# A 3x3 convolution on one core: two blocks in a turn of TensorE's loop, and the context ended ahead of the wait for the last stores

## The chip, the cores and the metric

The kernel runs on one core of a Trainium2 chip. The metric is the device time of one execution in microseconds (us); the figure for a kernel is the median of several runs. A profile is one execution recorded by the hardware profiler; its *span* runs from the first to the last recorded instruction, and the execution's own device time is a little longer than the span.

## The reference

A batch of 16 images with 64 channels of 64 x 64 points is convolved with 128 filters of 3 x 3, with one row and column of zeros around each image. Everything is float32 in memory.

```python
batch, c_in, h, w, c_out = 16, 64, 64, 64, 128
x_pad = np.pad(x, ((0, 0), (0, 0), (1, 1), (1, 1)), mode='constant')
output[b, co] += weight[co, ci, kh, kw] * x_pad[b, ci, kh:kh+h, kw:kw+w]   # over ci, kh, kw
```

The input is 16.8 MB, the output 33.6 MB.

## The kernel before

**Tiling.** Two images make a pair p (0 to 7): their 2 x 64 channels fill the 128 partitions. A pair is computed in four blocks of 16 output rows, so there are 32 blocks n = 4p + blk. The 16 output rows of a block are 8 even and 8 odd ones.

**The trick in the rows.** Along the rows, pairs of output rows share work. With the row taps g0, g1, g2 of the filter, the kernel keeps five weight sets in `Wt`: G1, and G0, G2, G21 = g2 - g1 and G01 = g0 - g1. For each block TensorE makes three groups of sums, each for both images (b2 = 0, 1), a bank of PSUM for each image:
- group 0 (shared): G1 on the sums of two neighbouring rows (`ss`), 3 column taps x 2 images = 6 matmuls;
- group 1 (even rows): G21 on one row set and G0 on the row above, 12 matmuls from `xs`;
- group 2 (odd rows): G01 and G2 (the row below), 12 matmuls from `xs`.

A matmul uses 64 of the 128 rows of the array, one image's channels, and those of the two images alternate. It has 8 rows x 64 columns, or 63 for the outer column taps. At an image's top G0 would read a row above it, at its bottom G2 one below; there, these six matmuls have 7 rows.

**The engines' parts.** TensorE (PE) runs the 30 matmuls of each block (L294). POOL makes the sums `ss` (L115; the first two blocks' by DVE). ACT copies group 0's banks to `ut` in SBUF (L204), then casts the rows of the next block to float16 in `xs` (L121). DVE adds `ut` to the even and the odd rows' banks and writes the float32 result (L234): four adds of 512 columns in a block, the even rows' (i = 0) for both images first, then the odd ones'. Finished pairs are stored from `homes`, one store for each image (2 MB) and two of 1 MB for the last pair's; image 0's by SP's queue, image 1's by ACT's (L109). Pairs 0 to 3 are loaded by SP as float32 into `homes`, pairs 4 to 7 by POOL's queue with a cast to float16 (L95), at points given by `LOADS`. Nine `homes` of 2 MB serve as inputs first and then as outputs, so a first add of a pair may have to wait for an earlier store (`gate_out`).

**The order.** It is written out by hand with semaphores. `s_pe`, `s_act` and `s_dve` count what the engines have finished; `tiles(n, k)` is the count at which the k-th bank of block n is done, `copies(n, k)` and `adds(n, k)` the like for ACT and DVE. TensorE alone runs a hardware loop (L263: 8 turns of four blocks, with `hint_back_edge=True`), and since a loop can't wait for growing counts it takes credits: `c_sum` (a block's sums), `c_cast` (its cast), `c_bank` (a pair of banks was read out by DVE: one after the even adds, one after the odd adds, except the last), each lowered by 1 at L273. `c_bank` starts at 3.

**The banks.** A block's six banks are `(6n + 2g + b2) % 8`, so groups walk in a ring of four pairs. Group 0 of block n takes the pair that the odd adds of block n-2 read, group 2 the one that the even adds of block n-1 read; group 1's pair was freed by ACT's copies ahead of `c_cast`.

**The places of rows and sums.** `xs` holds all 64 rows of a pair, `ss` 32 sums; a block's cast covers the rows of `CUTS` (18, 16, 16, 14 rows). POOL mostly sums two blocks in one instruction.

**The end.** Stores whose home is not used again count up `s_end`. After the critical section closes (L73), SP waits for `s_end` (L306), and then the context ends (L332): the engines meet in barriers, and POOL clears the range of semaphores.

Of the kernel before, what the change touches and what calls it, by code (L numbers as in the profile page):

```python
# [6 lines left out]
F16 = mybir.dt.float16  # L7

NP = 8
NB = 4  # L10
RB = 8
H = W = 64
CO = 128
TILES = 6
G0, G21, G1, G01, G2 = range(5)
# [3 lines left out]

PIECES = [(0, 32), (0,), (0,), (0,), (0,), (0,), (0, 32), (0, 32, 50)]  # L20

LOADS = {6: [(6, 0), (6, 1)], 8: [(7, 0)], 10: [(7, 1), (7, 2)]}
CUTS = [(0, 18), (18, 34), (34, 50), (50, 64)]


def kernel(tc: tile.TileContext, x: bass.AP, weight: bass.AP, out: bass.AP):
    nc = tc.nc
# [3 lines left out]
    def sem(name):  # L31
        return tc.alloc_semaphore(name)

    def sbuf(name, shape, dt):
        return nc.alloc_sbuf_tensor(name, shape, dt).ap()
# [3 lines left out]
    s_in = [[sem(f"s_in{p}{k}") for k in range(len(PIECES[p]))] for p in range(NP)]  # L39
    s_pe = sem("s_pe")  # L40
    s_act = sem("s_act")
    s_dve = sem("s_dve")
    s_out = {}
    s_end, s_done = sem("s_end"), sem("s_done")

    c_sum, c_cast, c_bank = sem("c_sum"), sem("c_cast"), sem("c_bank")

    def tiles(n, k):
        return 3 + TILES * n + k

    def copies(n, k):
        return 3 + 2 * n + k
# [6 lines left out]
    PE, ACT, DVE, POOL, SP = nc.tensor, nc.scalar, nc.vector, nc.gpsimd, nc.sync  # L59
# [10 lines left out]
    def when(inst, s, count):  # L70
        return inst.wait_op(s, count, "sem-ge")

    with tc.tile_critical(sync_engine=EngineType.Pool):  # L73
        homes = [sbuf(f"home{k}", [128, H, W], F32) for k in range(9)]
        pairs = homes[:4] + [sbuf(f"pair{p}", [128, H, W], F16) for p in range(4, NP)]
        xs = sbuf("xs", [128, H, W], F16)
        ss = sbuf("ss", [128, H // 2, W], F16)
        uts = [[sbuf(f"ut{k}{b}", [128, RB, W], F32) for b in range(2)] for k in range(2)]
        w_raw = sbuf("w_raw", [CO, 64 * 9], F32)
        w16 = sbuf("w16", [CO, 64 * 9], F16)  # L80
# [1 line left out]
        zeros = sbuf("zeros", [128, 512], F16)  # L82
        ident = sbuf("ident", [128, 128], F16)
        banks = [nc.alloc_psum_tensor(f"bank{k}", [128, RB, W], F32).ap() for k in range(8)]
# [5 lines left out]
        def rows(t):  # L90
            return t.rearrange("p (j i) c -> p j i c", i=2)

        def load(eng, p, k):
            lo, hi = (PIECES[p] + (H,))[k : k + 2]
            eng.dma_start(  # L95
                pairs[p][:, lo:hi, :], x_rows[128 * p : 128 * p + 128, lo:hi, :]
            ).then_inc(s_in[p][k], 16)
# [4 lines left out]
        def arrived(eng, name, p, hi):  # L102
            for k, lo in enumerate(PIECES[p]):
                if lo < hi and (name, p, k) not in seen:
                    seen.add((name, p, k))
                    eng.wait_ge(s_in[p][k], 16)
# [3 lines left out]
                out[2 * p + b2, :, lo:hi, :], homes[OUT_HOME[p][b2]][:, lo:hi, :]  # L110
            ).then_inc(s, 16)

        def sums(eng, lo, n, p):
            v = rows(pairs[p])
            return eng.tensor_add(  # L115
                ss[:, lo : lo + n, :], v[:, lo : lo + n, 0, :], v[:, lo : lo + n, 1, :]
            )

        def cast(m):
            lo, hi = CUTS[m % NB]  # L120
            return ACT.copy(xs[:, lo:hi, :], pairs[m // NB][:, lo:hi, :])  # L121


        gate_out = {}
        pieces, n_end = {}, 0
# [47 lines left out]
        when(POOL.tensor_copy(w16, w_raw), s_w, 16).then_inc(s_pool, 1)  # L173
        POOL.wait_ge(s_dve, 2).then_inc(c_sum, 1)
        POOL.wait_ge(s_dve, 3).then_inc(c_sum, 1)
        arrived(POOL, "pool", 0, H)
        load(POOL, 4, 0)
        sums(POOL, 2 * RB, 2 * RB, 0).then_inc(c_sum, 2)
        for k in range(2, 2 * NP):
            p = k // 2  # L180
            lo = 2 * RB * (k % 2)
            n = RB if k == 2 * NP - 1 else 2 * RB
            arrived(POOL, "pool", p, 2 * (lo + n))
            if k == 4:
                load(POOL, 5, 0)
            when(sums(POOL, lo, n, p), s_pe, tiles(2 * k - 3, 2)).then_inc(c_sum, n // RB)
            if n == RB:
                arrived(POOL, "pool", p, H)
                sums(POOL, lo + n, n, p).then_inc(c_sum, 1)
            for q, piece in LOADS.get(k, ()):  # L190
                load(POOL, q, piece)


        wp_bank = {G1: 4, G2: 5, G0: 6}
        for i, g in enumerate((G1, G2, G0)):
            when(
                ACT.copy(wrow(g), flat[wp_bank[g]][:, 0 : 3 * CO]), s_pe, i + 1  # L197
            ).then_inc(s_act, 1)
        arrived(ACT, "act", 0, CUTS[0][1])
        cast(0).then_inc(c_cast, 1)  # L200
        for n in range(NB * NP):
            for b2 in range(2):
                when(
                    ACT.copy(uts[n % 2][b2], banks[(6 * n + b2) % 8]), s_pe, tiles(n, 1 + b2)  # L204
                ).then_inc(s_act, 1)
            m = n + 1
            if m < NB * NP:
                arrived(ACT, "act", m // NB, CUTS[m % NB][1])
                cast(m).then_inc(c_cast, 1)
            done = n - 1  # L210
            if done >= 0 and (done // NB, 1, done % NB) in pieces:
                p = done // NB
                ACT.wait_ge(s_dve, adds(n, 1))
                store(ACT, p, 1, *pieces[p, 1, done % NB])
# [4 lines left out]
        DVE.memset(zeros, 0.0).then_inc(s_dve, 1)  # L219
        when(DVE.tensor_sub(wrow(G21), wrow(G2), wrow(G1)), s_act, 2)  # L220
        when(DVE.tensor_sub(wrow(G01), wrow(G0), wrow(G1)), s_act, 3)  # L221
        when(sums(DVE, 0, RB, 0), s_in[0][0], 16).then_inc(s_dve, 1)
        sums(DVE, RB, RB, 0).then_inc(s_dve, 1)
        for n in range(NB * NP):
            p, blk = divmod(n, NB)
            j0 = RB * blk
            for i in range(2):
                for b2 in range(2):
                    if blk == 0 and i == 0 and gate_out[p, b2] is not None:
                        DVE.wait_ge(*gate_out[p, b2])  # L230
                    if i == 0 and b2 == 0:
                        DVE.wait_ge(s_act, copies(n, 2))
                    add = when(
                        DVE.tensor_add(  # L234
                            rows(homes[OUT_HOME[p][b2]])[:, j0 : j0 + RB, i, :],
                            banks[(6 * n + 2 + 2 * i + b2) % 8],
                            uts[n % 2][b2],
                        ),
                        s_pe,
                        tiles(n, 3 + 2 * i + b2),  # L240
                    )
                    last = n == NB * NP - 1 and i == 1
                    add.then_inc(s_dve if b2 == 0 or last else c_bank, 1)
# [15 lines left out]
                    )  # L259
            mm.then_inc(s_pe, 1)  # L260
        spin(4)
        PE.sem_inc(c_bank, 3)
        with nc.Fori(0, NP, engines=(EngineType.PE,), hint_back_edge=True):  # L263
            for blk in range(NB):
                j0 = RB * blk
                groups = (
                    ([(G1, None)], (c_sum, c_bank)),
                    ([(G21, 1), (G0, -1)], (c_cast,)),
                    ([(G01, 0), (G2, 2)], (c_bank,)),
                )  # L270
                for gi, (taps, credits) in enumerate(groups):
                    for c in credits:
                        PE.wait_ge(c, 1).then_inc(c, -1)  # L273
                    acc = [banks[(6 * blk + 2 * gi + b2) % 8] for b2 in range(2)]
                    n = 3 * len(taps)
                    i = 0
                    for wi, off in taps:
                        for kw in (1, 0, 2):
                            c_lo, c_hi = max(0, 1 - kw), min(W, W + 1 - kw)
                            for b2 in range(2):  # L280
                                p0 = 64 * b2
                                lo, hi = j0, j0 + RB
                                cols = slice(c_lo + kw - 1, c_hi + kw - 1)
                                if off is None:
                                    rhs = ss[p0 : p0 + 64, lo:hi, cols]
                                else:
                                    while 2 * lo + off < 0:
                                        lo += 1
                                    while 2 * (hi - 1) + off > H - 1:
                                        hi -= 1  # L290
                                    rhs = xs[
                                        p0 : p0 + 64, 2 * lo + off : 2 * (hi - 1) + off + 1 : 2, cols
                                    ]
                                mm = PE.matmul(  # L294
                                    acc[b2][:, lo - j0 : hi - j0, c_lo:c_hi],
                                    Wt[p0 : p0 + 64, wi, kw, :],
                                    rhs,
                                    start=i == 0,
                                    stop=i == n - 1,
                                )  # L300
                                if i == n - 1:
                                    mm.then_inc(s_pe, 1)
                            i += 1

    tc.no_sync_barrier()
    SP.wait_ge(s_end, SP.to_reg(16 * n_end)).then_inc(s_done, 1)  # L306


# [28 lines left out]
```

## Time and profile before

| | |
|---|---|
| median of 3 runs | 126.46 us (126.23 to 126.65) |
| the profiled execution | 125.64 us |
| its span | 123.8 us |
| TensorE matmul busy | 108.0 us (87%) |
| DVE busy | 84.1 us (68%) |
| ACT busy | 67.2 us (54%) |
| POOL busy | 38.9 us (31%) |
| HBM read, written | 17.07 MB, 33.55 MB |

How to read the views: the rows of tenths cut the span in 40 slices of 3.1 us, a digit 9 being 90% or more. `PEclk` is the granted clock of TensorE. A row of groups has line, engine, operation, out<-in with shapes, number, and then busy time and the mean of one. A row of the timeline has the start, the length, the line and the number of instructions merged; the bracket tells the idle time before and what ended it. Rows with a q behind the engine (PEldq, SPq) are of its instruction sequencer. Matmuls overlap, so the length of a row of matmuls runs past the start of the next.

### The profile page before, as it was taken

Reading aid. Unit: us, or ns where it says so; the run is one execution under the profiler, and the core shown is the slowest. Engines: PE = TensorE matmul, PEld = TensorE weight load, DVE = VectorE, ACT = ScalarE, POOL = GpSimd, SP = SyncE. Lnnn points to the kernel's source line nnn. Section 1 sums busy time; section 2 is a strip of 40 time slices with the busy share of each in tenths; the row PEclk is TensorE's granted clock in tenths of the full one; section 3 lists DMA queues with packets and bytes.
Section 4 is the critical chain, followed back from the end, with each engine's and each line's share of the span. In section 5 each row is a group of like instructions: output and inputs, shape, how many; then the busy total and the mean of one; then the engine's idle time right before and its main releaser. Section 6 shows DMA issues by size and latency. Waiting matters only on the chain.

```text
span 123.8 us, 2533 instructions
## 1 busy us (share of the span) xinstructions
PE 108.0 (87%) x989; PEld 56.7 (46%) x989; DVE 84.1 (68%) x133; ACT 67.2 (54%) x100; POOL 38.9 (31%) x30
## 2 busy tenths in 40 slices
PE   5969999999999999999999999999999999970000
PEld 1525555555555555555555555555555555530000
DVE  0067777877787778777877787788888887771000
ACT  4266656666666666666666566656665666520000
POOL 2207457170708270615054423233241103000000
PEclk9999999999999999999999999999999999999555
DMA  4999999999999999999999999999999999999993
GB/s 108 392 442 424 365 320 326 387 296 363 365 352 344 381 396 379 392 380 389 387 392 377 388 387 381 380 395 413 383 400 412 422 383 429 432 426 416 429 426 156
DMA packets 4467, 46.46 MB, mean 375 GB/s; under 512 B 496, under 2 KB 624, under 8 KB 1264
## 3 DMA queue, kind: packets, MB, share of 16 engines
q1 hardware_dynamic: 2160, 25.46, 50.0%
q10 hardware_dynamic: 1296, 16.78, 31.7%
q0 software_dynamic: 1008, 4.19, 16.6%
q14 instruction: 3, 0.02, 0.0%
HBM read 17.07 MB, written 33.55 MB: 409 GB/s over the span
## 4 chain that ended last, share of the span: by engine, by line
PE 82%; DVE 2%; DVEq 0%; issue 0%
PE bank L294 82%; DVE home L234 2%; DVEq L73 0%
## 5 line engine op out<-in xcount | busy, mean ns | idle before, releaser
L234 DVE TENSOR_TENSOR home<-bank,ut 128x512 f32<-128x512 f32 x128 | 81.9, 686 | 21.9 <-PE bank L294 21.7
L294 PE MATMUL bank<-xs,Wt 64*128 64x504 f16 (+3 forms) x768 | 87.5, 373 | 0.0
L294 PEld LDWEIGHTS bank<-xs,Wt 64*128 64x128 f16 x768 | 43.6, 94 | 38.6
L204 ACT COPY ut<-bank 128x512 f32<-128x512 f32 x64 | 34.4, 589 | 37.7 <-PE bank L294 37.7
L115 POOL TENSOR_TENSOR ss<-pair 128x1024 f16<-128x1024 f16 (+1 forms) x9 | 17.1, 1906 | 39.1 <-PE bank L294 32.4
L294 PE MATMUL bank<-ss,Wt 64*128 64x504 f16 (+1 forms) x192 | 26.5, 377 | 1.1 <-PEq L273 1.1
L115 POOL TENSOR_TENSOR ss<-home 128x1024 f16<-128x1024 f32 x7 | 16.5, 2364 | 14.5 <-PE bank L294 12.5
L121 ACT CAST xs<-home 128x1024 f16<-128x1024 f32 (+2 forms) x16 | 16.9, 1057 | 0.3 <-DMA home<-in_x_dram 0.3
L121 ACT COPY xs<-pair 128x1024 f16<-128x1024 f16 (+2 forms) x16 | 16.9, 1059 | 0.0
L294 PEld LDWEIGHTS bank<-ss,Wt 64*128 64x128 f16 x192 | 10.8, 94 | 10.8 <-issue 1.5
L95 POOL DMA_DIRECT2D pair<-in_x_dram x7 | 4.0, 577 | 8.6 <-DMA home<-in_x_dram 8.6
L248 PE MATMUL bank<-zeros 128*128 128x512 f16 x11 | 4.2, 540 | 1.4 <-DVE zeros L219 1.4
L220 DVE TENSOR_TENSOR Wt<-Wt 128x384 f16<-128x384 f16 x1 | 0.4, 358 | 4.8 <-ACT Wt L197 4.8
L197 ACT CAST Wt<-bank 128x384 f16<-128x384 f32 x3 | 1.2, 487 | 3.1 <-PE bank L257 3.1
L248 PEld LDWEIGHTS bank<-zeros 128*128 128x128 f16 x11 | 1.2, 124 | 3.1 <-DVE zeros L219 1.4
L197 ACT ACT_TABLE_LOAD x1 | 1.3, 1283 | 0.9 <-PEq L321 0.9
L257 PEld LDWEIGHTS bank<-ident,w 128*64 128x64 f16 x18 | 1.1, 209 | 1.0 <-POOL w L173 1.0
L173 POOL CAST w<-w_raw 128x576 f16<-128x576 f32 x1 | 0.7, 662 | 2.4 <-DMA w_raw<-in_weight_dram 2.4
L257 PE MATMUL bank<-ident,w 128*64 128x128 f16 x18 | 1.3, 299 | 0.1
L115 DVE TENSOR_TENSOR ss<-home 128x512 f16<-128x512 f32 x2 | 1.3, 688 | 0.0
L219 DVE MEMSET zeros<- 128x256 uint32 x1 | 0.3, 272 | 1.1 <-PEq L321 1.1
L221 DVE TENSOR_TENSOR Wt<-Wt 128x384 f16<-128x384 f16 x1 | 0.4, 359 | 0.0
(6 smaller groups left out, 0.9 us busy)
## 6 DMA issues: line engine op xcount, KB each, us to landing
out_dram<-home SPq DMA_DIRECT2D x7, 2048.0 KB, 23.0
out_dram<-home ACTq DMA_DIRECT2D x7, 2048.0 KB, 18.2
home<-in_x_dram SPq DMA_DIRECT2D x3, 2048.0 KB, 21.2
home<-in_x_dram SPq DMA_DIRECT2D x2, 1024.0 KB, 6.5
pair<-in_x_dram POOLq DMA_DIRECT2D x2, 1024.0 KB, 16.8
out_dram<-home SPq DMA_DIRECT2D x2, 1024.0 KB, 11.6
out_dram<-home ACTq DMA_DIRECT2D x2, 1024.0 KB, 11.1
pair<-in_x_dram POOLq DMA_DIRECT2D x3, 512.0 KB, 29.3
```

The costliest lines, as they stand in the source:

```text
L95: eng.dma_start(pairs[p][:, lo:hi, :], x_rows[128 * p : 128 * p + 128, lo:hi, :]).then_inc(s_in[p][k], 16)
L115: return eng.tensor_add(ss[:, lo : lo + n, :], v[:, lo : lo + n, 0, :], v[:, lo : lo + n, 1, :])
L121: return ACT.copy(xs[:, lo:hi, :], pairs[m // NB][:, lo:hi, :])
L173: when(POOL.tensor_copy(w16, w_raw), s_w, 16).then_inc(s_pool, 1)
L197: ACT.copy(wrow(g), flat[wp_bank[g]][:, 0 : 3 * CO]), s_pe, i + 1
L204: ACT.copy(uts[n % 2][b2], banks[(6 * n + b2) % 8]), s_pe, tiles(n, 1 + b2)
L220: when(DVE.tensor_sub(wrow(G21), wrow(G2), wrow(G1)), s_act, 2)
L221: when(DVE.tensor_sub(wrow(G01), wrow(G0), wrow(G1)), s_act, 3)
L234: DVE.tensor_add(rows(homes[OUT_HOME[p][b2]])[:, j0 : j0 + RB, i, :], banks[(6 * n + 2 + 2 * i + b2) % 8], uts[n % 2][b2],),
L248: PE.matmul(flat[7], zeros[:, 0:128], zeros)
L257: mm = PE.matmul(flat[wp_bank[g]][q : q + 64, k * CO : k * CO + CO], w16[:, t::9], ident)
L294: mm = PE.matmul(acc[b2][:, lo - j0 : hi - j0, c_lo:c_hi], Wt[p0 : p0 + 64, wi, kw, :], rhs, start=i == 0, stop=i == n - 1,)
```

## The change

- **TensorE's loop** has 16 turns of two blocks (`slot` 0 and 1), and no hint for its back edge. All matmuls of `xs` have 8 rows.
- **Places.** `xs` has two places of 18 rows, `ss` two of 8 sums; block n uses place n % 2. A cast covers the block's 16 rows and one on either side; beyond an image's edge ACT writes a row of zeros.
- **POOL** sums one block in an instruction, waiting for group 0 of block n-2. The loads of pairs 6 and 7 stand behind the sums of blocks 11, 15 and 19, with a wait for the first piece of the next block's pair ahead of them.
- **Banks.** Group 1 always has banks 2 and 3, group 2 banks 4 and 5, group 0 alternates between 0, 1 and 6, 7. `c_bank` starts at 2; group 0 takes `c_sum` alone, group 1 `c_cast` and `c_bank`, group 2 `c_bank`.
- **The end.** `s_end` is allocated outside the context's own semaphores. The context is closed, then SP waits for `s_end` and clears it.

```diff
-LOADS = {6: [(6, 0), (6, 1)], 8: [(7, 0)], 10: [(7, 1), (7, 2)]}
-CUTS = [(0, 18), (18, 34), (34, 50), (50, 64)]
+LOADS = {11: [(6, 0), (6, 1)], 15: [(7, 0)], 19: [(7, 1), (7, 2)]}
...
-        xs = sbuf("xs", [128, H, W], F16)
-        ss = sbuf("ss", [128, H // 2, W], F16)
+        xs = sbuf("xs", [128, 2, 2 * RB + 2, W], F16)
+        ss = sbuf("ss", [128, 2, RB, W], F16)
...
+        def cast(n):
+            p, blk = divmod(n, NB)
+            lo, hi = 2 * RB * blk - 1, 2 * RB * blk + 2 * RB + 1
+            slot = xs[:, n % 2]
+            for edge, row in ((lo < 0, 0), (hi > H, 2 * RB + 1)):
+                if edge:
+                    ACT.copy(slot[:, row, :], zeros[:, 0:W])
+            r0, r1 = max(lo, 0), min(hi, H)
+            arrived(ACT, "act", p, r1)
+            return ACT.copy(slot[:, r0 - lo : r1 - lo, :], pairs[p][:, r0:r1, :])
+
+        def shared(n, b2):
+            return banks[6 * (n % 2) + b2]
...
+        for n in range(2, NB * NP):
+            p, blk = divmod(n, NB)
+            arrived(POOL, "pool", p, 2 * RB * (blk + 1))
+            if n == 2:
+                load(POOL, 4, 0)
+            if n == 8:
                 load(POOL, 5, 0)
...
+            when(sums(POOL, n), s_pe, tiles(n - 2, 2)).then_inc(c_sum, 1)
+            if n in LOADS:
+                arrived(POOL, "pool", (n + 1) // NB, 1)
+                for q, piece in LOADS[n]:
+                    load(POOL, q, piece)
...
-        PE.sem_inc(c_bank, 3)
-        with nc.Fori(0, NP, engines=(EngineType.PE,), hint_back_edge=True):
-            for blk in range(NB):
-                j0 = RB * blk
+        PE.sem_inc(c_bank, 2)
+        with nc.Fori(0, NB * NP // 2, engines=(EngineType.PE,)):
+            for slot in range(2):
                 groups = (
-                    ([(G1, None)], (c_sum, c_bank)),
-                    ([(G21, 1), (G0, -1)], (c_cast,)),
+                    ([(G1, None)], (c_sum,)),
+                    ([(G21, 1), (G0, -1)], (c_cast, c_bank)),
                     ([(G01, 0), (G2, 2)], (c_bank,)),
                 )
...
-                    acc = [banks[(6 * blk + 2 * gi + b2) % 8] for b2 in range(2)]
+                    acc = [banks[2 * gi + b2] if gi else shared(slot, b2) for b2 in range(2)]
...
-                                    while 2 * lo + off < 0:
-                                        lo += 1
-                                    while 2 * (hi - 1) + off > H - 1:
-                                        hi -= 1
...
+                                    r0 = 1 + off
+                                    rhs = xs[p0 : p0 + 64, slot, r0 : r0 + 2 * RB - 1 : 2, cols]
...
-    tc.no_sync_barrier()
-    SP.wait_ge(s_end, SP.to_reg(16 * n_end)).then_inc(s_done, 1)
+    tc.close()
+    tc.compile()
+    SP.wait_ge(s_end, 16 * n_end)
+    SP.sem_clear(s_end)
+    nc.release_semaphore(s_end)
```

More of the change, by code (lines that the diff above doesn't have):

```diff
@@ L43 @@
     s_out = {}
-    s_end, s_done = sem("s_end"), sem("s_done")
+    s_end = nc.alloc_semaphore("s_end")
     c_sum, c_cast, c_bank = sem("c_sum"), sem("c_cast"), sem("c_bank")
@@ L111, in store, with sums @@
             ).then_inc(s, 16)
[L113 to L121, printed above, removed]
+        def sums(eng, n):
+            p, blk = divmod(n, NB)
+            v = rows(pairs[p])[:, RB * blk : RB * blk + RB]
+            return eng.tensor_add(ss[:, n % 2], v[:, :, 0, :], v[:, :, 1, :])
+        def cast(n):
[10 more added lines that the diff above has]
+            return banks[6 * (n % 2) + b2]
         gate_out = {}
@@ L175 @@
         POOL.wait_ge(s_dve, 3).then_inc(c_sum, 1)
[L176 to L184, printed above, removed]
-                load(POOL, 5, 0)
[L186 to L191, printed above, removed]
+        for n in range(2, NB * NP):
+            p, blk = divmod(n, NB)
+            arrived(POOL, "pool", p, 2 * RB * (blk + 1))
+            if n == 2:
+                load(POOL, 4, 0)
+            if n == 8:
+                load(POOL, 5, 0)
+            when(sums(POOL, n), s_pe, tiles(n - 2, 2)).then_inc(c_sum, 1)
[3 more added lines that the diff above has]
+                    load(POOL, q, piece)
         wp_bank = {G1: 4, G2: 5, G0: 6}
@@ L198 @@
             ).then_inc(s_act, 1)
-        arrived(ACT, "act", 0, CUTS[0][1])
         cast(0).then_inc(c_cast, 1)
@@ L203 @@
                 when(
-                    ACT.copy(uts[n % 2][b2], banks[(6 * n + b2) % 8]), s_pe, tiles(n, 1 + b2)
+                    ACT.copy(uts[n % 2][b2], shared(n, b2)), s_pe, tiles(n, 1 + b2)
                 ).then_inc(s_act, 1)
[L206 to L209, printed above, removed]
+            if n + 1 < NB * NP:
+                cast(n + 1).then_inc(c_cast, 1)
             done = n - 1
@@ L221 @@
         when(DVE.tensor_sub(wrow(G01), wrow(G0), wrow(G1)), s_act, 3)
-        when(sums(DVE, 0, RB, 0), s_in[0][0], 16).then_inc(s_dve, 1)
-        sums(DVE, RB, RB, 0).then_inc(s_dve, 1)
+        when(sums(DVE, 0), s_in[0][0], 16).then_inc(s_dve, 1)
+        sums(DVE, 1).then_inc(s_dve, 1)
         for n in range(NB * NP):
@@ L235 @@
                             rows(homes[OUT_HOME[p][b2]])[:, j0 : j0 + RB, i, :],
-                            banks[(6 * n + 2 + 2 * i + b2) % 8],
+                            banks[2 + 2 * i + b2],
                             uts[n % 2][b2],
@@ L279 @@
                             c_lo, c_hi = max(0, 1 - kw), min(W, W + 1 - kw)
+                            cols = slice(c_lo + kw - 1, c_hi + kw - 1)
                             for b2 in range(2):
                                 p0 = 64 * b2
-                                lo, hi = j0, j0 + RB
-                                cols = slice(c_lo + kw - 1, c_hi + kw - 1)
                                 if off is None:
-                                    rhs = ss[p0 : p0 + 64, lo:hi, cols]
+                                    rhs = ss[p0 : p0 + 64, slot, :, cols]
                                 else:
-                                    while 2 * lo + off < 0:
-                                        lo += 1
-                                    while 2 * (hi - 1) + off > H - 1:
-                                        hi -= 1
-                                    rhs = xs[
-                                        p0 : p0 + 64, 2 * lo + off : 2 * (hi - 1) + off + 1 : 2, cols
-                                    ]
+                                    r0 = 1 + off
+                                    rhs = xs[p0 : p0 + 64, slot, r0 : r0 + 2 * RB - 1 : 2, cols]
                                 mm = PE.matmul(
-                                    acc[b2][:, lo - j0 : hi - j0, c_lo:c_hi],
+                                    acc[b2][:, :, c_lo:c_hi],
                                     Wt[p0 : p0 + 64, wi, kw, :],
```

## The prediction

> **What bounds the kernel now.** I read the page first, then the DMA share in stretches, then the timeline of the steady loop, then the last microsecond. The page:
>
> ```profile
> span 123.8 us, 2533 instructions
> PE   5969999999999999999999999999999999970000
> PEclk9999999999999999999999999999999999999555
> DMA  4999999999999999999999999999999999999993
> q1 hardware_dynamic: 2160, 25.46, 50.0%
> q10 hardware_dynamic: 1296, 16.78, 31.7%
> q0 software_dynamic: 1008, 4.19, 16.6%
> PE bank L294 82%; DVE home L234 2%; DVEq L73 0%
> ```
>
> Two resources look full: TensorE from slice 4 to slice 36, and the DMA engines from slice 2 to the end. The chain names TensorE for 82%, but its shares sum to 84%: it stops at about 111 us, and the rest of the span belongs to transfers. The three data queues took 50.0 + 31.7 + 16.6 = 98.3% of sixteen engines' span. The stretches (seconds column the length, then busy times, granted clock, DMA share, GB/s) say the same:
>
> ```profile
> 3.00:111.00 108.00, 106.43 (x986) 56.10 (x984) 82.95 (x131) 65.88 (x99) 38.22 (x24) 1.00 1.02 386
> 111.00:122.64 11.64, 0.00 (x0) 0.00 (x0) 0.85 (x2) 0.00 (x0) 0.00 (x0) 0.64 0.92 389
> 122.64:123.78 1.14, 0.00 (x0) 0.00 (x0) 0.00 (x0) 0.00 (x0) 0.00 (x0) 0.50 0.00 0
> ```
>
> From 3 us to the last landing there is no stretch in which the DMA engines ran out of work: the share is 1.02 while TensorE computes and 0.92 after it has stopped. So the transfers are one uninterrupted queue of work and their sum sets 122.64. Then 1.14 us follow in which neither DMA nor compute runs. I take the kernel as DMA-bound with a fixed tail, and TensorE as the second bound, some microseconds behind it.
>
> How many microseconds behind: the last store (ACT queue) is issued when DVE's last add is done, at 111.9 (chain: 109.36 + 1.90 = 111.26, and the queue shows a DMA issue of ACT last starting at 111.9). From there to 122.64 are 10.7 us, at 389 GB/s some 4.2 MB. The last two stores are 1.05 MB each, 2.1 MB; so about 2.1 MB, or 5.4 us, was older work. A transfer needs about 1 us from issue to first movement (estimate from w_raw, the first transfer: 3.0 us from issue to landing, of which its 0.29 MB need 0.8 at this rate; I put half of the other 2.2 ahead of the data). TensorE may be late by 5.4 - 1 = 4.4 us before an engine goes idle. I call this the cover.
>
> **TensorE: matmuls of seven rows become eight.** Before, the first block of a pair skips the row above the image, the last the row below: 64 + 32 = 96 matmuls of seven rows (441 or 448 columns). Afterwards all have eight. The timeline gives the price:
>
> ```profile
> 11.08 0.83 PE L294 MATMUL bank<-ss,Wt 64*128 64x512 f16 x6
> 13.22 2.58 DVE L234 TENSOR_TENSOR home<-bank,ut 128x512 f32<-128x512 f32 x4 [0.66 <-PE bank L294]
> 14.32 0.83 PE L294 MATMUL bank<-ss,Wt 64*128 64x512 f16 x6
> 14.75 2.49 PEld L294 LDWEIGHTS bank<-xs,Wt 64*128 64x128 f16 x24
> 14.97 2.77 PE L294 MATMUL bank<-xs,Wt 64*128 64x512 f16 x24
> 17.56 0.83 PE L294 MATMUL bank<-ss,Wt 64*128 64x512 f16 x6
> 20.72 0.83 PE L294 MATMUL bank<-ss,Wt 64*128 64x512 f16 x6
> ```
>
> A block of full matmuls takes 14.32 - 11.08 = 3.24 us, one with a cut edge 20.72 - 17.56 = 3.16. Sixteen edge blocks times 0.08 are 1.28 us more. They fit in the cover of 4.4 us, so: 0 to the end; without the cover +1.28.
>
> **Back edges: 15 instead of 7, and no hint.** The loop's own instructions on TensorE's sequencer:
>
> ```profile
> L263 PEldq ALU_OP  x8: 36/36/42, 18.5 to 108.1; - x8
> L263 PEldq COMPARE_BRANCH  x8: 88/223/241, 18.6 to 108.2; - x8
> ```
>
> A taken branch took 0.22 to 0.24 us, but the sequencer runs ahead: the first was at 18.6 while the array began the next turn at 20.72, and that turn's boundary (17.56 to 20.72) is no longer than the first block. Cost before: nothing. Afterwards the sequencer's lead shrinks, because its last wait of a block is for a credit (below) at about 1.5 us into it. It then issues 24 instructions and branches; even with 0.6 us for the issue it is back at 1.5 + 0.6 + 0.3 = 2.4 us of 3.24. Cost taken 0; uncovered, 15 x 0.3 = 4.5 us. The eight hints (0.03 us each) go from a sequencer that isn't the limit: 0.
>
> [...] The trace: the old body has 120 matmuls and 120 weight loads, the new one 60 and 60, and the page counts only three packets on the instruction queue (q14) in the span, against seven taken edges, so no edge fetched its body again; whether the hint did that, it can't show.
>
> **Banks: a tighter credit.** Before, the sums' group waits for DVE's second adds of two blocks earlier and the third group for the first adds of the block before. Now the second group waits for the first adds of the block before and the third for its second adds. In the rows above: block 1's four adds start at 13.22 and take 2.58, so the first two end at 14.51, the others at 15.80. Block 2's second group loads weights at 14.75; its third group starts at 14.97 + 1.27 = 16.24, its weights 0.22 earlier, 16.02. Slack 0.24 and 0.22 us. The hand-over from DVE to TensorE took 0.06 at the start (memset of zeros from 1.07 for 0.27, first weight load at 1.40). So 0.16 us is left; cost 0. Bounds: 0, and 0.2 per block (a hand-over of 0.43 us less the slack: so long after DVE's first sum, 6.84 + 0.65 = 7.49, came the loop's first matmul at 7.92, by way of POOL), 6.4 us. I take 0: the hand-over row is the nearest. What queues behind these waits is TensorE's stream alone.
>
> **ACT** casts 18 rows instead of 16, 17 and a zero row at the edges. The 18-row form took 1.165 us, 16 rows 1.058, 14 rows 0.95. Copies and cast come to 1.07 + 1.17 = 2.24, with a zero row (estimate 0.2, by the 0.83 ns per column between these forms plus a start) 2.4 of 3.24: hidden in ACT's 37.7 us of idle; the first zero row falls into the 0.3 us in which ACT waits for the first rows. The store that ACT issues behind its cast leaves as before.
>
> **POOL** makes 30 sums of one block (1.15 to 1.2 us) instead of double ones (2.12 to 2.36). A sum may start when the first group two blocks earlier is done, over 5 us ahead of need: 0. The loads of pairs 6 and 7 follow a sum that waits for the same matmul as before, behind one block's sum instead of two: about 1 us earlier, less 0.5 of TensorE's lateness. The added waits there (pairs 3, 4, 5) are for transfers landed long before; behind them stand only later sums. All other load issues stay. Same bytes, same queues, engines never idle: 0.
>
> **The end.** The rows of the exit, after the stores' wait:
>
> ```profile
> L306 SPq EVENT_SEMAPHORE  x1: 17/17/17, 122.6 to 122.6; - x1
> L332 SPq EVENT_SEMAPHORE  x4: 17/22/28, 122.7 to 123.7; - x4
> L332 POOLq EVENT_SEMAPHORE_RANGE_CLEAR  x1: 225/225/225, 123.3 to 123.3; - x1
> L332 PEldq EVENT_SEMAPHORE  x2: 51/51/51, 123.1 to 123.7; - x2
> ```
>
> After 122.64 come two rounds of barrier and a clearing of semaphores, to 123.78: 1.14 us. Now these run ahead of the wait, from about 113 on (SP's last store, 111.3 + 1.3, is what they wait for), under nine microseconds of transfers. Behind the wait stay the wait itself and one clear on SP: 2 x 0.02, with gaps of 0.08 as between SP's present ones, about 0.14. Saving 1.0. Bounds: 0.5, if one round stays behind; 1.3, if the 1.84 us outside the span (125.64 - 123.8) also shrink because four engines finish early.
>
> **Sum**: 123.8 + 0 + 0 + 0 - 1.0 = 122.8 us of span; with 1.84 around it 124.64. The median of the runs, 126.46, lies 0.82 above that profiled execution, so 126.46 - 1.0 = **125.45 us**. Own range: DMA sum +-0.3, tail 0.5 to 1.3: 124.8 to 126.2.
>
> **Rivals.** 1. Slower: the credit ring. If handing a bank back costs TensorE more than the 0.22 us of slack, each block is longer by the excess. It decides from (4.4 + 1.0 - 1.28) / 32 = 0.13 us of excess per block on. At 0.2 per block: 1.28 + 6.4 - 4.4 - 1.0 = +2.3, 128.7 us. For it: the third group's slack was 16.24 - 14.51 = 1.7 us and falls to 0.2. Against: the adds repeat to 0.01 us in every block, and a hand-over took 0.06. Chance 0.08.
> 2. [...] Chance 0.04.
> 3. No cover: TensorE's end sets the time after all, 126.46 + 1.28 - 1.0 = 126.74 us. For: the chain. Against: DMA share 0.92 to 1.02. Chance 0.05.
> 4. The end does not shorten, as something after the wait makes up for it: 126.45 us. Chance 0.06.
>
> **Chances.** The forecast keeps 0.77. The measurement tells 0.3% (0.4 us) from no change; faster then means below 126.08. Of the forecast 0.75 falls there, of rivals 3 and 4 together 0.02, of rival 1 (an excess just below its point) 0.01: 0.78. Within 0.3%: the other 0.09 of rivals 3 and 4 and 0.02 of the forecast, 0.11. Slower: the rest of rivals 1 and 2, 0.11. The range goes to 126.5, to take in rival 4.
>
> **What would show it.** Right: blocks all 3.24 us, TensorE's end 1.3 later than 110.5 (107.85 + 2.69); DMA share 1.0 up to the last landing near 122.6; L332's rows moved to 113; span about 122.8. Wrong: idle time ahead of the loop's matmuls put down to DVE (rival 1); instruction packets in the tens (rival 2); a last landing that moves by 1.28 (rival 3); rows after SP's last wait (rival 4).

## The result, and the profile after

The changed kernel took 125.09 us (median of 4 runs, 124.47 to 125.46) against 126.46 us; the ratio is 0.9891, with a 95% interval of 0.9863 to 0.9919. That is 1.4 us less, where 1.0 was forecast. Medians here are over all executions of a kernel; a ratio and its interval leave out those more than 1.5% above that kernel's fastest. The page of the profiled execution, which took 125.06 us by itself:

```profile
span 123.8 us, 2564 instructions
PE   5959999999999999999999999999999999992000
PEclk9999999999999999999999999999999999999555
DMA  3999999999999999999999999999999999999994
q8 instruction: 1, 0.02, 0.0%
q14 instruction: 3, 0.02, 0.0%
PE bank L290 84%; DVE home L237 1%; DVEq L73 0%
```

The span is the same 123.8 us as before. TensorE works into one slice more, and the chain names it for 84% instead of 82%, yet the execution was 0.6 us shorter: the part outside the span fell from 1.84 to 1.3 us. The stretches show how two changes of opposite sign make the equal span (length, busy times, granted clock, DMA share, GB/s):

```profile
3.00:111.00 108.00, 106.70 (x980) 56.23 (x980) 82.19 (x129) 70.81 (x115) 40.71 (x38) 1.00 1.02 385
111.00:122.64 11.64, 1.00 (x10) 0.30 (x6) 2.30 (x4) 0.00 (x0) 0.00 (x0) 0.66 0.95 400
122.64:123.78 1.14, 0.00 (x0) 0.00 (x0) 0.00 (x0) 0.00 (x0) 0.00 (x0) 0.50 0.05 22
```

The DMA engines are as full as before, but a trickle of transfers (share 0.05) goes on where the barriers stood. A store lands in 16 parts (496 landings of 31 transfers in either trace), and at the end those of the last two stores mix: from 122 us on, 4 packets of SP's queue (q1) move among 17 of ACT's (q10). By the landings in the trace, all but four parts had come by 122.84 (before: all by 122.63), and the last came at 123.71. The last landings of the other executions below without added lateness came between 122.8 and 123.7, with either loop and either end, so this end moves by about a microsecond from one execution to another, and one profile of each kernel does not tell the 1.08 us from chance.

The spans of the other executions do. The kernel before has a median span of 124.4 us in the 73 executions beside the experiments (123.7 to 126.2), the changed kernel 123.3 in its 11 (123.0 to 123.8). So the profile of the kernel before happened to be among its shortest and that of the changed kernel among its longest; by the medians the span became 1.1 us shorter. Taking off what stands behind the last landing in the two profiles (1.14 and 0.05 us) puts the usual last landing, as an estimate, at 123.3 with both kernels.

The steady loop, in the timeline (start, length, work):

```profile
11.33 0.83 PE L290 MATMUL bank<-ss,Wt 64*128 64x512 f16 x6
13.47 2.59 DVE L237 TENSOR_TENSOR home<-bank,ut 128x512 f32<-128x512 f32 x4 [0.66 <-PE bank L290]
14.57 0.83 PE L290 MATMUL bank<-ss,Wt 64*128 64x512 f16 x6
15.01 2.49 PEld L290 LDWEIGHTS bank<-xs,Wt 64*128 64x128 f16 x24
17.81 0.83 PE L290 MATMUL bank<-ss,Wt 64*128 64x512 f16 x6
21.06 0.83 PE L290 MATMUL bank<-ss,Wt 64*128 64x512 f16 x6
```

Every block takes 3.24 us now: 14.57 - 11.33, and also (3.25 by the rounded rows) 21.06 - 17.81, the edge block that took 3.16. The boundary at 14.57 is a back edge, the one at 17.81 is not; they do not differ. DVE's adds start 2.14 us into their block (13.47 - 11.33), as before (13.22 - 11.08).

The exit, by source line (engine, instruction, lengths, first and last start):

```profile
L304 POOLq EVENT_SEMAPHORE_RANGE_CLEAR  x2: 113/124/135, 114.7 to 115.0; - x2
L304 PEldq EVENT_SEMAPHORE  x2: 51/51/51, 114.6 to 115.4; - x2
L306 SPq EVENT_SEMAPHORE_RANGE_CLEAR  x1: 25/25/25, 123.7 to 123.7; - x1
```

The barriers and the clearing are over at 115.4, eight microseconds ahead of the last landing; behind it stands one clear of 25 ns.

### The profile page after: what moved, and what is told of

It reads as the page before. It is cut to its first block, busy times and chain, and to the rows that moved or that the text cites. A ratio compares the mean times of both kernels' runs of the same rounds, so it can differ in the third digit from the quotient of the medians.

```text
span 123.8 us, 2564 instructions
## 1 busy us (share of the span) xinstructions
PE 109.3 (88%) x989; PEld 57.1 (46%) x989; DVE 84.8 (68%) x133; ACT 72.1 (58%) x116; POOL 41.4 (33%) x44
## 4 chain that ended last, share of the span: by engine, by line
PE 84%; DVE 1%; DVEq 0%; issue 0%
PE bank L290 84%; DVE home L237 1%; DVEq L73 0%
## 5 line engine op out<-in xcount | busy, mean ns | idle before, releaser
L290 PE MATMUL bank<-xs,Wt 64*128 64x504 f16 (+1 forms) x768 | 88.8, 377 | 0.0
L117 POOL TENSOR_TENSOR ss<-pair 128x512 f16<-128x512 f16 x16 | 18.5, 1153 | 33.0 <-PE bank L290 33.0
L117 POOL TENSOR_TENSOR ss<-home 128x512 f16<-128x512 f32 x14 | 17.8, 1274 | 22.1 <-PE bank L290 22.1
L128 ACT CAST xs<-home 128x1088 f16<-128x1088 f32 (+1 forms) x16 | 18.2, 1138 | 0.6 <-DMA home<-in_x_dram 0.6
L128 ACT COPY xs<-pair 128x1088 f16<-128x1088 f16 (+1 forms) x16 | 18.2, 1139 | 0.0
L125 ACT COPY xs<-zeros 128x64 f16<-128x64 f16 x16 | 4.1, 258 | 0.0
```

What stands on the lines that cost most here:

```text
L117: return eng.tensor_add(ss[:, n % 2], v[:, :, 0, :], v[:, :, 1, :])
L125: ACT.copy(slot[:, row, :], zeros[:, 0:W])
L128: return ACT.copy(slot[:, r0 - lo : r1 - lo, :], pairs[p][:, r0:r1, :])
L290: mm = PE.matmul(acc[b2][:, :, c_lo:c_hi], Wt[p0 : p0 + 64, wi, kw, :], rhs, start=i == 0, stop=i == n - 1,)
```

## The experiments

Each median stands beside the runs of the kernel before that shared its chip.

**1. The end alone, and the loop alone.** One (e1_end) is the kernel before with the changed end, by the diff; the other (e2_loop) the changed kernel with the same lines the other way round.

```diff
-    s_end, s_done = sem("s_end"), sem("s_done")
+    s_end = nc.alloc_semaphore("s_end")
...
-    tc.no_sync_barrier()
-    SP.wait_ge(s_end, SP.to_reg(16 * n_end)).then_inc(s_done, 1)
+    tc.close()
+    tc.compile()
+    SP.wait_ge(s_end, 16 * n_end)
+    SP.sem_clear(s_end)
+    nc.release_semaphore(s_end)
```

> The kernel before with the new end alone. Transfers theory (the last landing is set by the sum of the transfers, TensorE's lateness is covered): the whole gain is here, 125.1 to 125.5 us, a span 0.8 to 1.1 us shorter than before's at an equal last landing. Rival (TensorE's end sets the time, and the gain of the end is partly eaten by the 1.28 us of matmuls): the new end without them is faster still, about 123.9 us.

> The changed kernel with the old end: barriers and clearing behind the wait for the last stores. Transfers theory: as before, 126.3 to 126.6 us, though TensorE ends 1.3 to 1.5 us later. Rival (TensorE's end sets the time): 127.7 us.

Measured: e1_end 124.57 us against 126.39, ratio 0.986 (0.984 to 0.988). e2_loop 126.35 us, ratio 0.9994 (0.9974 to 1.0014). So the whole gain belongs to the end, and the loop's part changes nothing that can be told. TensorE's row of the chain (start, length, work) in e1_end:

```profile
7.90 101.44 PE bank L294 x948
```

And in e2_loop:

```profile
7.67 103.94 PE bank L290 x960
```

TensorE's part is 2.50 us longer. Of these, some 1.2 us are 12 more matmuls of the last block, and only mean that the chain leaves TensorE one group later; the other 1.3 us are the edge blocks. With the old end they cost nothing. The rival's 127.7 us for the loop alone lies outside the interval; e1_end came out between the two expectations, and the gain of the end is larger than I had put it.

**2. The changed kernel and the end alone on one chip.** Both once more, without an edit.

> The changed kernel once more, to stand beside the kernel before with the new end alone on one chip. If the loop's 1.3 us of lateness is wholly covered, the two agree within 0.3 us; if it passes on in part, this one is 0.3 to 1.3 us slower.

> The kernel before with the new end alone once more: 124.4 to 124.8 us.

Measured: 124.74 us (0.9854, 0.9825 to 0.9883) and 124.98 us (0.9872, 0.9832 to 0.9912), before 126.45. They agree within 0.3 us, though the end alone came 0.2 us above the range expected for it. A third run of the end alone, on another chip, was 124.97 (experiment 6). The gain of the new end is thus 1.5 to 1.8 us in three comparisons of medians, not 1.0. The spans tell where it lies: medians of 123.1, 123.05 and 123.2 with the new end alone, against 124.3, 124.3 and 124.2 of the kernel before on the same chips. So 1.0 to 1.25 us of it are in the span, the rest outside.

**3. How late may TensorE be?** The changed kernel with 18 more idle matmuls ahead of TensorE's loop (e3_late18, the first part of the diff); then, beside that, the stores of pair 6 cut in two (e7_late18_cut, both parts).

```diff
-        spin(4)
+        spin(22)
...
-                cuts = [(3, 0, H)] if p < NP - 1 else [(1, 0, 32), (3, 32, H)]
+                cuts = [(3, 0, H)] if p < NP - 2 else [(1, 0, 32), (3, 32, H)]
```

> The changed kernel with 18 more idle matmuls ahead of TensorE's loop, at some 0.22 us each; 1.26 us of them fall into the wait for the first sums, so every block comes 2.7 us later, and the last store some 4.1 us later than in the kernel before. Transfers theory (cover 4.4 us): within 0.3 us of the changed kernel, about 125.1. Rival (TensorE's end sets the time): about 127.8 us.

Measured: 126.65 us (125.76 to 129.51), ratio 0.9989 (0.9957 to 1.0022). The expectation of my theory failed: the lateness took back the whole gain. The rival's 127.8 us did not come either. The stretches of e3_late18 around pair 6's first store:

```profile
99.00:101.00 2.00, 2.00 (x22) 0.88 (x18) 1.34 (x3) 1.69 (x4) 1.16 (x1) 1.00 1.00 426
101.00:102.00 1.00, 1.00 (x14) 0.47 (x10) 0.99 (x3) 0.53 (x1) 0.00 (x0) 1.00 0.74 311
102.00:103.00 1.00, 1.00 (x12) 0.41 (x10) 1.00 (x2) 0.45 (x1) 0.37 (x1) 1.00 0.16 66
103.00:104.00 1.00, 1.00 (x12) 0.49 (x10) 0.34 (x2) 1.00 (x3) 0.79 (x1) 1.00 0.66 279
```

The row of that store in its timeline, on SP's queue:

```profile
102.62 0.33 SPq L110 DMA_DIRECT2D out_dram<-home  x1
```

The DMA share falls to 0.16 although TensorE never pauses: the stores of pair 5 and the loads are done, and pair 6's 2 MB are not yet there. In the kernel before, this store was issued at 98.48, in the changed kernel at 99.77 (their timelines, two stores merged in each row):

```profile
98.48 6.74 SPq L109 DMA_DIRECT2D out_dram<-home  x2
99.77 6.82 SPq L110 DMA_DIRECT2D out_dram<-home  x2
```

It is 4.1 us late in e3_late18, and the engines lost 0.26 + 0.84 + 0.34 = 1.4 us. So the cover at this place is 2.7 us, of which the changed kernel uses 1.3 and leaves 1.4. I had worked out 4.4 us, at the last stores, ten microseconds later.

> The late kernel (18 more idle matmuls) with the stores of pair 6 cut in two, so that the first halves leave two blocks (6.5 us) earlier. If the lateness broke through at pair 6's stores, where the DMA share fell to 0.16 for a microsecond: no such gap, and 1 to 1.7 us less than without the cut, about 125.1 us. If it broke through at the last stores: no change, 126.2 to 126.7 us.

Measured: 126.37 us (125.11 to 130.23), ratio 0.9942 (0.9909 to 0.9976). The same stretches of e7_late18_cut, and its last microseconds:

```profile
101.00:102.00 1.00, 1.00 (x12) 0.48 (x10) 0.99 (x3) 0.24 (x1) 0.00 (x0) 1.00 0.93 395
102.00:103.00 1.00, 1.00 (x14) 0.45 (x10) 0.91 (x2) 0.73 (x2) 0.65 (x1) 1.00 1.00 426
103.00:104.00 1.00, 1.00 (x12) 0.43 (x10) 0.43 (x1) 1.00 (x2) 0.50 (x1) 1.00 1.03 428
122.00:126.00 4.00, 0.00 (x0) 0.00 (x0) 0.00 (x0) 0.00 (x0) 0.00 (x0) 0.50 0.07 29
```

The hole at 102 is closed, as the theory has it, but the time came back in part only: by the ratios 0.5%, 0.6 us, on different chips and with intervals that overlap a little. In this profile the rest is in the last stretch: all but four parts of the last stores had landed at 122.76, these four at 123.3 to 125.0. Why they run late is not shown, and these two kernels' times vary more than the others'.

**4. The back edge.** The hint put back in the changed kernel (e4_hint), and taken from the kernel before (e8_old_nohint).

```diff
-        with nc.Fori(0, NB * NP // 2, engines=(EngineType.PE,)):
+        with nc.Fori(0, NB * NP // 2, engines=(EngineType.PE,), hint_back_edge=True):
...
-        with nc.Fori(0, NP, engines=(EngineType.PE,), hint_back_edge=True):
+        with nc.Fori(0, NP, engines=(EngineType.PE,)):
```

> The changed kernel with the hint for the back edge. If the unhinted edge costs nothing (the blocks across an edge take 3.24 us as the others do): unchanged, 124.8 to 125.4 us, blocks 3.24 us. If the edge costs 0.1 us or more that the cover hides: TensorE's end comes 1.5 us or more sooner at an equal time.

> The kernel before without the hint for its back edge; its body has 120 matmuls, 120 weight loads and 16 waits. If a body of that size stays at hand without a hint: unchanged, 126.3 to 126.5 us, blocks 3.16 and 3.24 us. [...]

Measured: e4_hint 124.77 us, ratio 0.9869 (0.9847 to 0.9891); e8_old_nohint 126.85 us, ratio 1.002 (0.9993 to 1.0047). By the time, neither can be told from its fellow, though e8_old_nohint's median lies 0.35 us above the range expected for it. In the timeline of e8_old_nohint, the block ahead of its first back edge and the one behind it begin at:

```profile
18.32 0.83 PE L294 MATMUL bank<-ss,Wt 64*128 64x512 f16 x6
21.48 0.83 PE L294 MATMUL bank<-ss,Wt 64*128 64x512 f16 x6
```

The instruction queues on its page (packets, MB, share):

```profile
q8 instruction: 1, 0.02, 0.0%
q14 instruction: 2, 0.02, 0.0%
```

The edge block takes 21.48 - 18.32 = 3.16 us, as with the hint, and so do the other six; TensorE's part of the chain is 101.44 us for 948 matmuls, as in e1_end, which has the hint. The page counts three instruction packets in the span, against seven taken edges. So no edge held TensorE up. A taken branch lasted 0.21 to 0.24 us with the hint and without, and was over before the array began the next turn: the first began at 19.3 here, the turn at 21.48; in the changed kernel at 13.1, the turn at 14.57. The spans of e8_old_nohint are longer than those of the kernel before on its chip (median 125.0 against 124.3). In its profile the blocks are no longer, but the loop's first matmul starts at 8.68 instead of 7.92, and the last landing comes at 123.55; whether the missing hint has to do with that is not shown.

**5. The tighter credit.** One more operation on DVE in each block, between the two even adds, in the changed kernel and in the kernel before. It writes places that nothing reads.

```diff
+        spare = sbuf("spare", [128, 512], F32)
...
+                    if i == 0 and b2 == 1:
+                        DVE.memset((spare, w_raw[:, 0:512])[n % 2], 0.0)
                     add = when(
```

> The changed kernel with one more operation on DVE in each block, a memset of 128 x 512 float32 between the two even adds (about 0.5 us by the 0.27 of the one of half as many words), which sends both credits that much later. By the slack of 0.16 to 0.24 us the blocks grow by about 0.3 us to 3.5 to 3.6, TensorE ends some 10 us later, and the time comes to 131 to 134 us. If the credits had more room than that: blocks 3.24 us, about 125.1.

> The kernel before with the same operation on DVE. Its credits have 1.7 us of slack, and DVE's four adds and the memset fit in a block of 3.24 us: blocks unchanged, 126.2 to 126.6 us. If DVE's own time decided instead of the credits, it would grow like the changed kernel.

Measured: e9_ring_new 128.45 us against 126.6, ratio 1.0125 (1.0048 to 1.0203); e10_ring_old 126.75, ratio 1.0004 (0.9977 to 1.0032), 0.15 us above the range expected for it. In e9_ring_new's timeline:

```profile
20.94 0.48 DVE L238 MEMSET w_raw<- 128x512 f32 x1
21.29 0.83 PE L293 MATMUL bank<-ss,Wt 64*128 64x512 f16 x6
22.09 1.01 PEld L293 LDWEIGHTS bank<-xs,Wt 64*128 64x128 f16 x12 [0.46 <-issue]
24.71 0.83 PE L293 MATMUL bank<-ss,Wt 64*128 64x512 f16 x6
```

The weight loads of the second group now wait 0.46 us, and a block takes 24.71 - 21.29 = 3.42 us. In e10_ring_old blocks stay at 3.16 and 3.24; one with a cut edge, in its timeline (3.17 by the rounded rows):

```profile
17.38 0.83 PE L297 MATMUL bank<-ss,Wt 64*128 64x512 f16 x6
20.55 0.83 PE L297 MATMUL bank<-ss,Wt 64*128 64x512 f16 x6
```

So the two bank schemes do differ: the same 0.48 us of DVE is free in the old one and costs 0.17 us a block in the new one. The direction was as expected, the size was not: 0.48 less 0.17 leaves 0.31 us of room, where I had 0.16 to 0.24, and the time was 128.45 us, not 131 to 134. The stretches of e9_ring_new show once more where lateness breaks through:

```profile
102.00:103.00 1.00, 1.00 (x12) 0.58 (x11) 0.73 (x2) 0.96 (x1) 0.00 (x0) 1.00 0.13 49
103.00:104.00 1.00, 1.00 (x12) 0.34 (x6) 1.00 (x3) 0.00 (x0) 0.00 (x0) 1.00 0.00 0
104.00:105.00 1.00, 1.00 (x11) 0.48 (x10) 1.00 (x2) 0.84 (x2) 0.76 (x1) 1.00 0.00 0
105.00:106.00 1.00, 1.00 (x12) 0.58 (x10) 0.55 (x2) 1.00 (x2) 0.39 (x1) 1.00 0.62 262
```

The row of pair 6's store on SP's queue there:

```profile
104.61 0.33 SPq L111 DMA_DIRECT2D out_dram<-home  x1
```

Pair 6's store comes at 104.61, 6.1 us later than in the kernel before, and the engines lose 0.87 + 1 + 1 + 0.38 = 3.25 us: a cover of 2.9 us, at the same place.

**6. What the end gains outside the span.** e1_end with a barrier of all engines behind the wait, beside the same kernel without it.

```diff
     SP.sem_clear(s_end)
+    nc.all_engine_barrier()
```

> The kernel before with the new end, and one more barrier of all engines behind the wait for the last stores. The barrier itself costs the span some 0.25 us. If what the new end gains outside the span (1.84 us before, 1.26 in the changed kernel's profiled execution) comes from four engines being through long before the last landing, that goes too: 0.6 to 0.8 us slower than without the barrier. If it does not hang on them: 0.25 us slower.

> The kernel before with the new end alone, beside the one with the barrier: 124.4 to 125.0 us.

Measured: 125.49 us (0.9922, 0.9896 to 0.9948) with the barrier, 124.97 us (0.9888, 0.9845 to 0.9931) without, before 126.52. By the medians the barrier costs 0.5 us, with intervals that overlap; the rows of its lines in the trace, from SP's clear at 122.8 to the last release at 123.0, explain about half.

Every execution's span stands on record beside its time, and the two readings can be held against all of them. On this chip the time outside the span did not grow: 1.78 us (median) with the barrier, 1.97 without, while the span grew from 123.2 to 123.75. That speaks against the first reading. For it speak the smallest values. With the old end, none of 107 executions spent less than 1.73 us outside its span; with the new end, 44 of 61 did (2 of the 7 on this chip); with the barrier behind it, none of 8. So it stays open what the time outside the span hangs on.

## Why the prediction was right, and where it was not

- **Bound by transfers: right.** 1.28 us more of TensorE cost nothing (e2_loop, 0.9974 to 1.0014), and rival 3's 126.74 us did not come. Two of the signs named for this did not show in the profile of the changed kernel: its span was 123.8 us instead of 122.8, and its last landing 1.08 us later, close to the sign named for rival 3. The sum had started from a profile of the kernel before that was among its shortest; by the medians of all executions the span fell by 1.1 us, where 1.0 was forecast.
- **Edge blocks: right.** 3.24 us in every block, 16 x 0.08 us.
- **Back edges: right**, at nothing, with and without the hint: 3.24 us in the blocks across the edges of the changed kernel, and even the old body of 120 matmuls and 120 weight loads, without a hint, took no longer at its edges (3.16 us in e8_old_nohint). No run shows the slower edge that rival 2's chance of 0.04 stood for. The sequencer was also less pressed than worked out: it took its first branch 1.8 us into the block (13.1 against 11.33), not 2.4.
- **Credits: right in sign, off in size.** No stall in the changed kernel; the room was 0.31 us, not 0.16 to 0.24. The step counted the weight loads' normal lead as indispensable; with the credit late, the loop of e9_ring_new ran with 0.03 us of it instead of 0.21.
- **ACT and POOL: right.** Neither appears as something that TensorE waited for. The zero row took 0.26 us instead of 0.2, a sum from float32 rows 1.27 instead of 1.15 to 1.2.
- **The cover: wrong.** The step that failed is the one that counted the older bytes at the last store, and took 4.4 us from them. The backlog is smallest earlier, at pair 6's first store: 2.7 and 2.9 us in two kernels. The forecast held all the same, as the change makes TensorE late by only 1.3 us there; that the wrong figure did no harm was luck.
- **The end: right in mechanism, off in size.** 1.0 us was taken for the work behind the wait. The rows of L304 did move under the transfers, and rival 4 fell. In the span it was as worked out: 1.14 us of barriers and clearing against 0.05 now, and medians of spans that are 1.0 to 1.25 us shorter. But the end alone was worth 1.5 to 1.8 us, more than the 1.3 that I had as its upper bound. The rest, 0.2 to 0.6 us, is outside the span, where I took nothing for it. What it is made of was not settled.
- **The number.** The forecast of 125.45 us (by its own terms 125.46) was 0.36 us too high, on the side on which the end was taken too small.

No version here was clearly faster than the changed kernel: the end alone, without the new loop, equals it.

## What to carry to other kernels

When transfers fill the whole span, ask at every point how much queued work is left if the engine that feeds them is late; here the smallest backlog decided, 2.7 to 2.9 us at pair 6's first store, and not the 4.4 worked out at the last. What the engines did behind the last wait was added to the time: 1.1 us of barriers and clearing, which did not need the last landing and could be moved ahead of that wait. A bank scheme can be free in the trace and still have used up most of the slack: an extra operation of 0.48 us on DVE showed that 0.31 us of it was left here. One profile is one execution: here two profiles had equal spans of 123.8 us, where the medians were 124.4 and 123.3, and last landings 1.08 us apart; ask the other executions before explaining such a difference.

## What the runs showed that I had not expected

- The last parts of the stores do not land together: the last sixteen landings spread over 0.5 us in the kernel before, 1.5 us in the changed one, 3.0 us in the late one with pair 6's stores cut. The spans, which end at the last landing or 1.1 us behind it, are as uncertain as that here: 123.0 to 123.8 us in the 11 executions of the changed kernel.
- TensorE did with less lead for its weights: held back by a credit, a group's weight loads began 0.03 us ahead of its first matmul (22.09 and 22.12 in e9_ring_new) instead of 0.21 (15.01 and 15.22 in the changed kernel).
